# Split weight blocks at 17 start places, a backward and an alternating up projection in a two-layer encoder kernel

## The chip, the cores and the metric

The kernel runs on one core of a Trainium2 chip. Its time is the device time of one execution in microseconds, and lower is better. TensorE (PE) multiplies matrices, VectorE (DVE) and ScalarE (ACT) do elementwise work, GpSimd (POOL) a few memory sets, and SyncE (SP) issues the transfers.

## The reference

A trunk of two layers works on 512 tokens of width 1024, all in fp32. The first layer mixes tokens with differential attention, the second with chunked gated linear attention (GLA); beside it each layer attends to 256 memory tokens. Each layer ends with a gated MLP, which is where most of the change lies:

```python
def conv_ffn(h, w_up, conv_w, conv_b, w_down):
    u = h @ w_up                      # 1024 -> 2 * 2816
    c = depthwise causal convolution of width 3 over the tokens of u, + conv_b
    a, g = jnp.split(c, 2, axis=-1)
    return (jax.nn.silu(g) * a) @ w_down
...
for i in range(DEPTH):
    h = rms_norm(x, attn_norm[i])
    ...
    x = x + jnp.concatenate([mix, cross], axis=-1) @ w_out[i]
    h = rms_norm(x, ffn_norm[i])
    x = x + conv_ffn(h, w_up[i], conv_w[i], conv_b[i], w_down[i])
```

## The kernel before, in words

Everything is kept transposed: a tile has 128 features as partitions and the 512 tokens as columns, so an activation of width 1024 is eight tiles (k-tiles). Below, the first layer is `l = 0` in the code, the second `l = 1`.

**Split operands.** Each fp32 operand is written as a high part (rounded to the type float32r) and a low part (what is left), and a product is the sum of three matmuls: high by high, high by low, low by high. For weights, ACT casts the loaded block `raw` to `whi` (L253) and DVE subtracts to get `wlo` (L256); activations are split likewise into `xsh` and `xsl`.

**Weights as blocks.** All weights lie in DRAM as one row of blocks of 128 x 1024 or less, in the order of use. `_pieces` lists the pieces: four blocks for 512 columns of a projection, two for 256 columns of an up projection, three for 256 columns of a down projection over half of the hidden features. Three `raw` buffers are filled ahead by SP. The split parts have `WB` = 6 buffers each (L33, L286 and L474 for the first piece). `weights(key)` (L298) splits blocks so that the piece asked for and the one after it are there; in the projections `by_block` limits it to `WB` blocks, and `freed` (L307) splits one more when the last reader of a block has been issued.

**Two kinds of product.** In the projections of the token mixers (`gemm`, L330 to L332) the activation is the stationary operand and the weight block streams, 512 columns or 272. In the up, down and output projections (`product`, L351 to L353) 128 columns of the weight block are stationary and the 512 tokens of an activation stream into one PSUM bank: 8, 12 or 10 k-tiles of three matmuls each. PSUM has eight banks, two for each of the tags mm, sm, lg and tp.

**The MLP** (`ffn`, L1096). The 22 pairs of up tiles (a and g) are done in two halves of 6 and 5 weight pairs `q`, each with `n` = 0 and 1. For each `n`: the product a, the product g, then for both the convolution (`conv`, L1110: DVE L1111 empties the bank into `u`, ACT L1113, DVE L1114 and L1115), the silu (ACT L1146), the product of both (DVE L1147) and its split (ACT L1149, DVE L1150) into `midh` and `midl`. The tiles with n = 0 use the banks mm, those with n = 1 the banks sm. After the up tiles of a half come its eight down products over 12 or 10 mids, in their order, into banks lg and tp, each added to the residual (L1061).

**What sets the order.** TensorE keeps the order in which the code calls it; a hand-written script puts the units of the projections between the steps of attention. The order of ACT, DVE and SP is made by a scheduler at build time from dependencies and estimated costs and is then fixed: an instruction that waits holds all that stand behind it on its engine. A tile of a pool with all buffers in use waits until the readers of one of them are done.

Of the kernel before, what the change touches and what calls it, by code (L numbers as in the profile page):

```python
# [12 lines left out]
F32R = mybir.dt.float32r  # L13
# [16 lines left out]
WTILE = 1024  # L30
HALVES = (6, 5)
XS = 36
WB = 6  # L33

TOGETHER = (((0, 2), (0, 0)), ((0, 3),), ((0, 1), (1, 1)), ((1, 2), (1, 0)), ((1, 3),))
NT = 3 * len(TOGETHER)
# [143 lines left out]
def trunk(ctx, tc, head_d, x_t, mem_t, wpack, cols_a_d, cols_d, conv_d, gate_d, rel_bias, diff_lambda, consts, onehot, out):  # L180
# [86 lines left out]
    order = [(i, len(b[2]), b[4]) for i, piece in enumerate(blocks) for b in piece]  # L267
    first_of = [sum(len(q) for q in blocks[:i]) for i in range(len(blocks) + 1)]
    done, raw_q = [0], deque()

    def ahead():
        while len(raw_q) < 3 and done[0] + len(raw_q) < len(order):
# [3 lines left out]
    def make_block(raws=None):  # L276
        i, n, w = order[done[0]]
        if raws is None:
            ahead()
            raw = raw_q.popleft()  # L280
        else:
            raw = raws.pop(0)
        done[0] += 1
        while len(made) <= i:
            made.append([])
        hi, lo = (wp.tile([128, WTILE], F32R, name=t, tag=t, bufs=WB) for t in ("whi", "wlo"))  # L286
        split_weights(slice(0, n * w), raw, hi, lo, i == 2)
        made[i] += [(hi[:, blk(j, w)], lo[:, blk(j, w)]) for j in range(n)]
        if raws is None:
            ahead()  # L290
# [26 lines left out]
    def gemm(sh, sl, nb, key, w, evac, hook=None, late=False):  # L317
# [24 lines left out]
        for b, k in units:  # L342
            F.add(6 * w / 2370.0, lambda b=b, k=k: unit(b, k, k + 2))


    def product(p, parts, n, pairs, ids=None):
        ids = range(len(parts)) if ids is None else ids
        first, last = (ids[0], ids[-1]) if len(ids) == len(parts) else (0, len(parts) - 1)
        for i in ids:
            (hi, lo), (bh, bl) = parts[i], pairs[i]  # L350
            mm(p, hi[:, blk(n)], bh, start=i == first, stop=False)  # L351
            mm(p, hi[:, blk(n)], bl, start=False, stop=False)  # L352
            mm(p, lo[:, blk(n)], bh, start=False, stop=i == last)  # L353
# [83 lines left out]
    with tc.tile_pool(name="ini", bufs=1) as ip, tc.manual_schedule(engines={E.Activation, E.DVE, E.Pool, E.SP}):  # L437
        idle = ip.tile([128, 512], F32, name="idle")
        rb = ip.tile([32, 6], F32, name="rb")
        oh = ip.tile([32, 640], F32, name="oh")  # L440
        bs = xtile()[:6], xtile()[:6, :128]
        lv = xtile()[:, :256]
        G.memset(idle, 0.0)
        p = bank("tp")
        for n in (512, 320):
            mm(p[:, :n], idle[:, 0:128], idle[:, :n], start=True, stop=True)


        raws = [ip.tile([128, WTILE], F32, name=f"raw{i}") for i in range(4)]
        for t in (blk(0, S // 2), blk(1, S // 2)):  # L450
            A.dma_start(raws[0][:, t], wpack[0, :, t])
        head = ip.tile([128, 32 + S], F32, name="head")
        for c in (slice(0, 32 + S // 2), slice(32 + S // 2, 32 + S)):
            load(head[:, c], head_d[:, c])
        xT[0] = head[:, 32:]
        for k in range(1, KT):
            xT[k] = xtile()
            load(xT[k], x_t[k])
            load(raws[k // 2][:, blk(k % 2, S)], wpack[k // 2, :, blk(k % 2, S)])
        load(cols_a, cols_a_d)  # L460
        at[0] = 4
        load(C[:, 384:512], consts[:, 384:512])
        load(rb, rel_bias)
        load(oh, onehot)
        second = [load_raw(raw_tile(), WTILE) for _ in range(3)]
        load(cols, cols_d)
        load(lv, diff_lambda[0].rearrange("a b -> (a b)").partition_broadcast(128))
        parts, acc, split_w = [], [None], [None]
        made.append(parts)
        done[0] = 4  # L470

        def operands(k):
            if k % 2 == 0:
                split_w[0] = [wp.tile([128, WTILE], F32R, name=n, tag=n, bufs=WB) for n in ("whi", "wlo")]  # L474
            c = blk(k % 2, S)
            hi, lo = split_w[0]
            xh[k], xl[k] = split_tiles()
            if k == 0:
                for t in (blk(0, S // 2), blk(1, S // 2)):
                    V.tensor_copy(hi[:, t], raws[0][:, t])  # L480
                V.tensor_sub(lo[:, c], raws[0][:, c], hi[:, c].bitcast(F32))
                for t in (blk(0, S // 2), blk(1, S // 2)):
                    split(xh[0][:, t], xl[0][:, t], xT[0][:, t], col(0, head))
            else:
                split(xh[k], xl[k], xT[k], col(k, head))
                split_weights(c, raws[k // 2], hi, lo)
            parts.append((hi[:, c], lo[:, c]))
            squares(xT[k], acc)

        operands(0)  # L490
        for k in range(KT):
            if k + 1 < KT:
                operands(k + 1)
            if k == 0:
                second.append(load_raw(raws[0], WTILE))
            if k == 4:
                bias_rows(rb, oh, bs)
            if k == KT - 2:
                for j in range(4):
                    if j == 3:  # L500
                        token_rsqrt("lg", acc[0], NB, r_x[:, 0])
                    make_block(second)
                weights(("qk", 0), True)
                small_vectors()
                for c in range(2):
                    load(bias_d[:, 512 * c:min(512 * c + 512, 640)], bs[c])
            hi, lo = parts[k]
            terms = (xh[k], hi), (xh[k], lo), (xl[k], hi)
            full, left, right = slice(0, S), blk(0, S // 2), blk(1, S // 2)
            todo = [(b, i, full) for b in range(NB) for i in range(3)]  # L510
            if k == 0:
                todo = [(0, 0, left), (1, 0, left), (0, 0, right), (1, 0, right)] + sorted(
                    [u for u in todo if u[:2] not in ((0, 0), (1, 0))], key=lambda u: u[1])
            for b, i, t in todo:
                xp, w = terms[i]
                mm(first[b][:, t], xp[:, blk(b)], w[:, t], start=k == 0 and i == 0 and t is not right,
                   stop=k == KT - 1 and i == 2)
# [578 lines left out]
    def ffn(pool, l, acc):  # L1096
# [6 lines left out]
        def up(parts, n):  # L1103
            i = nu[0]
            nu[0] += 1
            p = bank("mm" if i % 4 < 2 else "sm")
            product(p, parts, n, list(zip(xh, xl)))
            return p, us[i % 4]

        def conv(p, u, j):  # L1110
            V.tensor_mul(u[:, 2:], p, rB)  # L1111
# [21 lines left out]
        for half, nq in enumerate(HALVES):  # L1133
            mids = []
            for q in range(base, base + nq):
                wa = weights(("ua", l, q))
                wg = None
                for n in range(2):
                    ua = up(wa, n)
                    wg = wg or weights(("ug", l, q))  # L1140
                    ug = up(wg, n)
                    if q == 0 and n == 0:
                        row_scales(acc[0])
                    ca = conv(*ua, 2 * q + n)
                    cg = conv(*ug, 22 + 2 * q + n)
                    A.activation(cg, cg, AF.Silu)  # L1146
                    V.tensor_mul(ca, ca, cg)  # L1147
                    mh, ml = split_tiles() if len(mids) < 5 else split_tiles(pool, "mid", 18)
                    A.copy(mh, ca)  # L1149
                    V.tensor_sub(ml, ca, mh.bitcast(F32))  # L1150
                    mids.append((mh, ml))
            last = half == 1
            if last and l == 0:
                tables("natural_log_exp_and_others")
            acc2 = [None]
            for c in range(4):
                pn = bank("lg"), bank("tp")
                parts = weights(("dn", l, base, c))
                for n in range(2):
                    product(pn[n], parts, n, mids)  # L1160
                for n in range(2):
                    if last and l == 1 and c == 3 and n == 1:
                        for t, queue in ((blk(0, S // 2), nc.sync), (blk(1, S // 2), nc.scalar)):
                            V.tensor_add(xT[7][:, t], xT[7][:, t], pn[n][:, t])
                            queue.dma_start(out[7, :, t], xT[7][:, t])
                        continue
                    update(2 * c + n, pn[n], (lambda k: c_attn(1, k)) if last and l == 0 else None, acc2)
                    if last and l == 0:
                        nc.sync.dma_start(xres[2 * c + n], xT[2 * c + n])
                    if last and l == 1:  # L1170
                        nc.sync.dma_start(out[2 * c + n], xT[2 * c + n])
            base += nq
# [88 lines left out]
```

## Time and profile before

| | |
|---|---|
| median of 2 runs | 1168.76 us (1168.76 to 1168.77) |
| profiled execution, first to last instruction | 1166.9 us |
| TensorE busy, matmuls | 1161.2 us, 5658 records |
| weight loads | 966.0 us |
| VectorE busy | 750.8 us |
| ScalarE busy | 545.6 us |
| bytes moved by the DMA queues | 117.68 MB, a mean of 101 GB/s |

The median lies 1.9 us above the span of the profiled execution, which counts from its first to its last instruction. Rows of a group read: line, engine, operation, output and inputs with their sizes, count, then busy time and mean duration of one in ns, then idle time before it. Rows of the timeline read: start, duration in us, engine, line, operation, tiles, count, and in brackets the idle time before it and what ended it. Rows of the windows read: stretch, its length, then busy time and count for PE, weight loads, DVE, ACT and POOL, the granted clock, the DMA share and GB/s. Plain fp32 matmuls have two records each.

### The profile page before, as it was taken

How to read it: one execution, taken by the hardware profiler on the slowest of the kernel's cores; microseconds unless marked ns; L12 is line 12 of the kernel's file. 1: busy time of each engine (PE TensorE's matmuls, PEld its weight loads, DVE VectorE, ACT ScalarE, POOL GpSimd, SP SyncE). 2: the span in 40 equal slices, each digit the busy share in tenths (PEclk: the TensorE clock that was granted, in tenths of full speed). 3: DMA queues.
4: the chain of work that ended last, by engine and by line, in shares of the span. 5: the costliest groups of instructions: out<-in, count | busy, mean ns of one | idle time of the engine just before them, and what ended most of it. 6: DMA issues, size and time to landing. Idle time of an engine off the chain costs nothing.

```text
span 1166.9 us, 14790 instructions
## 1 busy us (share of the span) xinstructions
PE 1161.2 (100%) x5658; PEld 966.0 (83%) x5658; DVE 750.8 (64%) x1256; ACT 545.6 (47%) x951; POOL 5.0 (0%) x27
## 2 busy tenths in 40 slices
PE   9999999999999999999999999999999999999998
PEld 7888888888888888888888888988888888888887
DVE  7576778688677326677447637777876743576741
ACT  6676787555344213344437634436643421343420
POOL 0000000000000000000000000000000000000000
PEclk9999999999999999999999999999999999999999
DMA  8522242234223223223341230333232333232231
GB/s 292 160 73 96 77 140 73 59 106 128 88 90 115 86 90 121 78 91 99 120 147 63 84 106 6 108 122 110 93 123 73 95 104 108 81 118 73 88 102 45
DMA packets 39556, 117.68 MB, mean 101 GB/s; under 512 B 4703, under 2 KB 7192, under 8 KB 39486
## 3 DMA queue, kind: packets, MB, share of 16 engines
q1 hardware_dynamic: 39054, 116.35, 30.9%
q8 instruction: 44, 0.72, 0.3%
q10 hardware_dynamic: 432, 0.39, 0.1%
q14 instruction: 26, 0.21, 0.1%
HBM read 112.52 MB, written 4.21 MB: 100 GB/s over the span
## 4 chain that ended last, share of the span: by engine, by line
PE 98%; ACT 1%; DVE 1%; issue 0%; POOL 0%; DVEq 0%; POOLq 0%
PE ps_mm L351 9%; PE ps_mm L352 9%; PE ps_mm L353 9%; PE ps_sm L352 8%; PE ps_sm L351 7%; PE ps_sm L353 7%; PE ps_mm L330 6%; PE ps_mm L332 6%; PE ps_mm L331 6%; PE ps_tp L351 3%; PE ps_lg L352 3%; PE ps_tp L352 3%; PE ps_lg L351 3%; PE ps_tp L353 3%; PE ps_lg L353 3%; PE ps_tp L220 3%
## 5 line engine op out<-in xcount | busy, mean ns | idle before, releaser
L253 ACT CAST whi<-raw 128x1024 fp32r<-128x1024 f32 (+4 forms) x212 | 207.7, 986 | 245.7 <-PE ps_tp L352 120.9
L256 DVE TENSOR_TENSOR wlo<-raw,whi 128x1024 fp32r<-128x1024 f32 (+4 forms) x212 | 240.3, 1139 | 117.6 <-ACT whi L253 116.7
L351 PE MATMUL ps_mm<-xsh,whi 128*128 128x512 f32 x438 | 171.6, 392 | 0.0
L353 PE MATMUL ps_mm<-xsh,wlo 128*128 128x512 f32 x438 | 170.5, 389 | 0.0
L352 PE MATMUL ps_mm<-xsl,whi 128*128 128x512 f32 x438 | 170.5, 389 | 0.0
L351 PE MATMUL ps_sm<-xsh,whi 128*128 128x512 f32 x378 | 147.0, 389 | 0.0
L352 PE MATMUL ps_sm<-xsl,whi 128*128 128x512 f32 x378 | 147.0, 389 | 0.0
L353 PE MATMUL ps_sm<-xsh,wlo 128*128 128x512 f32 x378 | 147.0, 389 | 0.0
L330 PE MATMUL ps_mm<-whi,xsh 128*128 128x512 f32 (+2 forms) x336 | 129.3, 385 | 0.0
L332 PE MATMUL ps_mm<-whi,xsl 128*128 128x512 f32 (+2 forms) x336 | 126.2, 375 | 0.0
L331 PE MATMUL ps_mm<-wlo,xsh 128*128 128x512 f32 (+2 forms) x336 | 125.8, 375 | 0.0
L1113 ACT ACTIVATE cvo<-u,cv 128x512 f32<-128x512 f32 x88 | 71.4, 815 | 112.1 <-DVE u L1111 112.1
L353 PEld LDWEIGHTS ps_mm<-xsh,wlo 128*128 128x128 f32 x438 | 82.2, 188 | 17.2
L351 PEld LDWEIGHTS ps_mm<-xsh,whi 128*128 128x128 f32 x438 | 82.2, 188 | 17.1 <-issue 0.3
L352 PEld LDWEIGHTS ps_mm<-xsl,whi 128*128 128x128 f32 x438 | 82.3, 188 | 17.0 <-DVE xsl L311 0.4
L1114 DVE SCALAR_TENSOR_TENSOR cvo<-u,cv,cvo 128x512 f32<-128x512 f32 x88 | 65.7, 748 | 36.2 <-ACT cvo L1113 36.0
L351 PEld LDWEIGHTS ps_sm<-xsh,whi 128*128 128x128 f32 x378 | 71.0, 188 | 14.8
L353 PEld LDWEIGHTS ps_sm<-xsh,wlo 128*128 128x128 f32 x378 | 71.0, 188 | 14.7
L352 PEld LDWEIGHTS ps_sm<-xsl,whi 128*128 128x128 f32 x378 | 71.0, 188 | 14.6
L332 PEld LDWEIGHTS ps_mm<-whi,xsl 128*128 128x128 f32 x336 | 63.2, 188 | 11.7
L330 PEld LDWEIGHTS ps_mm<-whi,xsh 128*128 128x128 f32 x336 | 63.2, 188 | 11.3 <-issue 0.3
L331 PEld LDWEIGHTS ps_mm<-wlo,xsh 128*128 128x128 f32 x336 | 63.3, 188 | 10.4
(295 smaller groups left out, 1760.8 us busy)
## 6 DMA issues: line engine op xcount, KB each, us to landing
raw<-in_wpack_dram SPq DMA_DIRECT2D x178, 512.0 KB, 3.5
xt<-in_x_t_dram SPq DMA_DIRECT2D x15, 256.0 KB, 5.4
raw<-in_wpack_dram SPq DMA_DIRECT2D x15, 256.0 KB, 3.1
raw<-in_wpack_dram SPq DMA_DIRECT2D x8, 384.0 KB, 3.1
xres<-xt SPq DMA_DIRECT2D x8, 256.0 KB, 2.7
xt<-xres SPq DMA_DIRECT2D x8, 256.0 KB, 6.2
out_dram<-xt SPq DMA_DIRECT2D x7, 256.0 KB, 2.0
bt<-bias_d SPq DMA_DIRECT2D x6, 256.0 KB, 4.4
```

Source lines behind the costliest of these rows:

```text
L220: nc.tensor.transpose(dst, src, ident[:n, :n])
L253: ins = A.copy(hi[:, c], raw[:, c])
L256: V.tensor_sub(lo[:, c], raw[:, c], hi[:, c].bitcast(F32))
L330: mm(p, sh[k][:, blk(b)], hi, start=k == 0, stop=False)
L331: mm(p, sh[k][:, blk(b)], lo, start=False, stop=False)
L332: mm(p, sl[k][:, blk(b)], hi, start=False, stop=k == KT - 1)
L351: mm(p, hi[:, blk(n)], bh, start=i == first, stop=False)
L352: mm(p, hi[:, blk(n)], bl, start=False, stop=False)
L353: mm(p, lo[:, blk(n)], bh, start=False, stop=i == last)
L1113: A.activation(c, u[:, 2:], AF.Identity, scale=cv[l][:, 2, j:j + 1], bias=cv[l][:, 3, j:j + 1])
L1114: V.scalar_tensor_tensor(c, u[:, 1:S + 1], cv[l][:, 1, j:j + 1], c, op0=ALU.mult, op1=ALU.add)
```

## The change

It does four things. The split parts of each weight block lie in a tile of 1024 + 64 columns and begin at one of 17 columns in turn (0, 4, ... 64, that is 16 bytes apart), the same place for `whi` and `wlo`. `WB` falls from 6 to 5. In the second layer the up tiles with n = 1 (a and g) read each streamed operand from its last token to its first and write the bank in the same reversed order, so that each result lands where it did. In the first layer the a and g products with n = 1 are issued together: for each k-tile and each of the three terms the matmul of a, then that of g, into the two banks sm in turn.

```diff
-WB = 6
+WB = 5
+PLACES = tuple(4 * i for i in range(17))
...
+    places = cycle(PLACES)
+
+    def weight_tiles():
+        c = next(places)
+        return [wp.tile([128, WTILE + max(PLACES)], F32R, name=n, tag=n, bufs=WB)[:, c:c + WTILE] for n in ("whi", "wlo")]
...
-        hi, lo = (wp.tile([128, WTILE], F32R, name=t, tag=t, bufs=WB) for t in ("whi", "wlo"))
+        hi, lo = weight_tiles()
...
+    def back(t):
+        return t[:, ::-1]
+
+    def product_back(p, parts, n, pairs):
+        for i in range(len(parts)):
+            (hi, lo), (bh, bl) = parts[i], pairs[i]
+            mm(back(p), hi[:, blk(n)], back(bh), start=i == 0, stop=False)
+            mm(back(p), hi[:, blk(n)], back(bl), start=False, stop=False)
+            mm(back(p), lo[:, blk(n)], back(bh), start=False, stop=i == len(parts) - 1)
+
+    def products(p2, parts2, n, pairs):
+        for i in range(len(pairs)):
+            bh, bl = pairs[i]
+            for t, x in ((0, bh), (0, bl), (1, bh)):
+                for p, parts in zip(p2, parts2):
+                    mm(p, parts[i][t][:, blk(n)], x, start=i == 0 and t == 0 and x is bh,
+                       stop=i == len(pairs) - 1 and t == 1)
...
-            product(p, parts, n, list(zip(xh, xl)))
+            if l == 1 and n == 1:
+                product_back(p, parts, n, list(zip(xh, xl)))
+            else:
+                product(p, parts, n, list(zip(xh, xl)))
             return p, us[i % 4]
+
+        def up2(parts, n):
+            i = nu[0]
+            nu[0] += 2
+            p = [bank("mm" if i % 4 < 2 else "sm") for _ in range(2)]
+            products(p, parts, n, list(zip(xh, xl)))
+            return [(p[0], us[i % 4]), (p[1], us[i % 4 + 1])]
...
-                    ua = up(wa, n)
-                    wg = wg or weights(("ug", l, q))
-                    ug = up(wg, n)
+                    if l == 0 and n == 1:
+                        ua, ug = up2((wa, wg), n)
+                    else:
+                        ua = up(wa, n)
+                        wg = wg or weights(("ug", l, q))
+                        ug = up(wg, n)
```

The first piece's tiles (L474) come from `weight_tiles` as well.

More of the change, by code (lines that the diff above doesn't have):

```diff
@@ L473, in operands @@
             if k % 2 == 0:
-                split_w[0] = [wp.tile([128, WTILE], F32R, name=n, tag=n, bufs=WB) for n in ("whi", "wlo")]
+                split_w[0] = weight_tiles()
             c = blk(k % 2, S)
```

## The prediction

> **What bounds the kernel now.** I read the page first (busy time, clock, the chain that ended last), then the groups, then the timeline of TensorE and of the engines that feed it.
>
> ```profile
> span 1166.9 us, 14790 instructions
> ...
> PE 1161.2 (100%) x5658; PEld 966.0 (83%) x5658; DVE 750.8 (64%) x1256; ACT 545.6 (47%) x951; POOL 5.0 (0%) x27
> ...
> PEclk9999999999999999999999999999999999999999
> ...
> PE 98%; ACT 1%; DVE 1%; issue 0%; POOL 0%; DVEq 0%; POOLq 0%
> ...
> L351 PE MATMUL ps_mm<-xsh,whi 128*128 128x512 f32 x438 | 171.6, 392 | 0.0
> ...
> L353 PEld LDWEIGHTS ps_mm<-xsh,wlo 128*128 128x128 f32 x438 | 82.2, 188 | 17.2
> ```
>
> TensorE is busy for the whole span, the chain lies on it for 98%, and it is granted its full clock throughout. So the time is the number of matmuls times the step from one start to the next, plus the few places where TensorE waits. The duration of 392 ns is not that step, because matmuls overlap; the step comes from starts in the timeline. The weight load of 188 ns lies beside the matmul before it.
>
> ```profile
> 299.62 0.39 PE L352 MATMUL ps_sm<-xsl,whi 128*128 128x512 f32 x1
> ...
> 305.97 0.39 PE L353 MATMUL ps_sm<-xsh,wlo 128*128 128x512 f32 x1
> ...
> 374.65 0.39 PE L353 MATMUL ps_sm<-xsh,wlo 128*128 128x512 f32 x1
> 374.88 0.39 PE L351 MATMUL ps_lg<-xsh,whi 128*128 128x512 f32 x1
> ...
> 613.30 0.29 PE L330 MATMUL ps_lg<-whi,xsh 128*128 128x272 f32 x1
> ...
> 616.20 0.29 PE L332 MATMUL ps_lg<-whi,xsl 128*128 128x272 f32 x1
> 616.32 0.46 PE L330 MATMUL ps_mm<-whi,xsh 128*128 128x512 f32 x1
> ...
> 728.01 0.82 PE L1015 MATMUL ps_sm<-gv,xt 128*128 128x192 f32 x4
> 728.66 0.49 PE L1017 MATMUL ps_sm<-st,qx 96*128 96x192 f32 x2
> ...
> 803.00:1109.00 306.00, 306.00 (x1352) 253.38 (x1351) 197.87 (x247) 125.10 (x153) 0.00 (x0) 1.00 0.30 95
> ```
>
> From 299.62 to 305.97 stand 29 matmuls of 512 columns, 28 steps: 6.35/28 = 0.227 us each. The last row is the second layer's MLP up to its last up tile: 306/1352 = 0.226 us, so nothing but that step is in it. The 24 matmuls of 272 columns from 613.30 to 616.32 give 0.126 us. Two widths give a line: (227 - 126)/240 = 0.42 ns a column, and 227 - 512 x 0.42 = 12 ns that do not depend on the width. Four plain fp32 matmuls of 192 columns take 0.65 us from 728.01 to 728.66, 0.163 us each, 0.85 ns a column: the slowest streaming rate that this trace shows, twice the split operands' 0.42.
>
> **The change, part by part.** The count of matmuls, weight loads, casts, subtractions and transfers is unchanged; starts, directions and order move.
>
> *Seventeen start places.* Every split block starts 0 to 256 bytes into a tile 256 bytes longer. I take nothing for it. For whi as streamed operand the 272-wide blocks already start at 0, 272 and 544 columns, odd multiples of 64 bytes, and keep the one step of 0.126 us. For whi as stationary operand no row shows an odd start; the load's 188 ns may grow by 39 ns before it fills the step of 227. Below nothing lie at most the 12 ns of every product matmul; above, a load of double length, 376 - 227 = 149 ns on each of 3552, 529 us, to which I give no chance, because the same columns of the same partitions are read. Nearest is the 272-wide row: no change. Casts and subtractions write to shifted starts on engines that are 47% and 64% busy.
>
> *Backwards in the second layer.* The second 128 columns of each up tile, 11 pairs x 2 products x 8 k-tiles x 3 terms = 528 matmuls, read the moving operand and write the bank from the last column to the first. No matmul before does so. Below nothing: 528 x 12 ns = 6 us of gain. Above: the rate of the 192-wide row, 0.42 ns more for each of 512 columns, 215 ns, x 528 = 114 us. I take nothing: neighbours in the bank and in SBUF still follow each other, only in the other order, and the nearest row is the forward matmul of the same shape. Both ends go into the range or the rivals.
>
> The Trainium skill ("PSUM — Partial Sum Buffer", Specifications) states that any non-contiguous access pattern slows matmuls significantly, because PSUM's lines are 8 bytes. Whether a step of minus one counts as that, it does not say; if it does, the sum is the upper end above, and no run yet shows it.
>
> *Alternating in the first layer.* In the 11 up tiles with n = 1, the a and g products become one run of 48 matmuls that change bank at every step. At 374.65 to 374.88 the bank changes, and the step is 0.23 us as ever: alternation itself costs and brings nothing. What it moves is the end of the a product: it ends with g's, 5.4 us (24 x 0.227) later. Both banks of tag sm ended their last tiles two products, 10.9 us, before, so the start is not held. In the middle of an MLP half nothing waits for the tile; at the end of a half the down projection needs it 33 matmuls later (12 mids, the last one third to wait) and in the second half 27 later.
>
> ```profile
> 374.89 1.05 ACT L253 CAST whi<-raw 128x1024 fp32r<-128x1024 f32 x1 [1.71 <-PE ps_sm L352]
> 375.87 0.82 ACT L1113 ACTIVATE cvo<-u,cv 128x512 f32<-128x512 f32 x1
> ...
> 375.08 0.69 DVE L1111 TENSOR_TENSOR u<-ps_sm,rB 128x512 f32<-128x512 f32 x1 [0.17 <-PE ps_sm L353]
> 375.98 1.23 DVE L256 TENSOR_TENSOR wlo<-raw,whi 128x1024 fp32r<-128x1024 f32 x1 [0.21 <-ACT whi L253]
> 377.12 0.75 DVE L1114 SCALAR_TENSOR_TENSOR cvo<-u,cv,cvo 128x512 f32<-128x512 f32 x1
> 377.91 0.75 DVE L1115 SCALAR_TENSOR_TENSOR cvo<-u,cv,cvo 128x512 f32<-128x512 f32 x1
> 379.36 0.69 DVE L1147 TENSOR_TENSOR cvo<-cvo 128x512 f32<-128x512 f32 x1 [0.70 <-ACT cvo L1146]
> ...
> 380.08 0.62 ACT L1149 CAST midh<-cvo 128x512 fp32r<-128x512 f32 x1 [0.76 <-DVE cvo L1147]
> ...
> 380.73 0.69 DVE L1150 TENSOR_TENSOR midl<-cvo,midh 128x512 fp32r<-128x512 f32 x1 [0.69 <-ACT midh L1149]
> ...
> 382.36 0.39 PE L351 MATMUL ps_lg<-midh,whi 128*128 128x512 f32 x1
> 382.58 0.39 PE L352 MATMUL ps_lg<-midl,whi 128*128 128x512 f32 x1
> ...
> 548.98 0.62 ACT L253 CAST whi<-raw 128x512 fp32r<-128x512 f32 x1 [1.71 <-PE ps_sm L352]
> 549.95 0.82 ACT L1113 ACTIVATE cvo<-u,cv 128x512 f32<-128x512 f32 x1 [0.35 <-DVE u L1111]
> ...
> 550.80 0.75 DVE L1114 SCALAR_TENSOR_TENSOR cvo<-u,cv,cvo 128x512 f32<-128x512 f32 x1 [0.35 <-ACT cvo L1113]
> ...
> 553.76 0.62 ACT L1149 CAST midh<-cvo 128x512 fp32r<-128x512 f32 x1 [0.76 <-DVE cvo L1147]
> ...
> 554.41 0.69 DVE L1150 TENSOR_TENSOR midl<-cvo,midh 128x512 fp32r<-128x512 f32 x1 [0.69 <-ACT midh L1149]
> ...
> 555.08 0.39 PE L351 MATMUL ps_lg<-midh,whi 128*128 128x512 f32 x1
> 555.30 0.40 PE L352 MATMUL ps_lg<-midl,whi 128*128 128x512 f32 x1
> ```
>
> Today a's convolution is done while g streams, and only g's is left: midl is ready at 381.42, needed at 382.58, a margin of 1.2 us; in the second half ready at 555.10, needed at 555.30, 0.2 us. After the change both stand behind the last up matmul. In the built program's order ACT then runs two weight casts (their buffers come free at that moment) ahead of the first convolution, and DVE runs two L1111, a subtraction, four convolution steps, a subtraction, L1147 and L1150.
>
> First half: the casts issue every 0.98 us (374.89 to 375.87), so the first convolution starts at 376.85 and ends at 377.67; L1114 starts 0.6 us later than at 377.12. Two more convolution steps add 2 x 0.77 = 1.5. Ahead of L1147 the second subtraction (about 1.15) takes the place of the 0.70 wait for the silu: 0.45. Together 2.6: midh ready at 383.3 for 382.36, a stall of 0.9; then midl at 384.0, when TensorE wants it at 383.5: 0.5 more. 1.4 us. Second half: two casts of 1024 columns from 548.98 put the convolution at 550.94, 1.0 us after 549.95; again 1.5 and 0.45, together 3.0: midh ready at 557.4 for 555.08, a stall of 2.3, and 0.5 for midl. 2.8 us. The second layer's MLP keeps its order there and its zero stall. Sum: 4.2 us; 0 to 7 if those offsets were all hidden or the subtractions fell worse.
>
> *Five buffers for six.* A block's cast waits for a release that is one block later; behind a waiting cast stand ACT's softmax exponentials, evacuations and convolutions, and behind those the tiles that TensorE needs. By the built order the shortest way from a release to the first use of the block that now takes the buffer is 25 matmuls. Its tightest place is in the second layer's projections:
>
> ```profile
> 641.82 0.39 PE L332 MATMUL ps_mm<-whi,xsl 128*128 128x512 f32 x1
> ...
> 645.26 2.03 ACT L253 CAST whi<-raw 128x1024 fp32r<-128x1024 f32 x2
> ...
> 646.40 2.35 DVE L256 TENSOR_TENSOR wlo<-raw,whi 128x1024 fp32r<-128x1024 f32 x2
> ...
> 647.73 0.39 PE L331 MATMUL ps_mm<-wlo,xsh 128*128 128x512 f32 x1
> ```
>
> The release is at 641.82, ACT gets to the cast at 645.26 behind the softmax, half of the pair of subtractions ends at 647.6, and the low part is wanted at 647.73. It just holds: I take nothing, with up to 3 us if such places miss by some tenths. In the MLP the shortest way is 40 matmuls, 9 us, against some 3 for cast and subtraction.
>
> Sum: 1166.9 + 4.2 = 1171.1 for the span. The median of the runs, 1168.76, lies 1.9 above that span; 1171.1 + 1.9 = 1173.0.
>
> **The rivals.**
> - *Backwards streaming runs at the slower rate.* Place: 528 matmuls of the second layer's MLP; price 215 ns each. It decides against my forecast from 36 ns a matmul on (19 us beside the 4.2, the 2% mark). 1173 + 114 = 1287. For it: no row shows a reversed pattern. Against: same neighbours, same line. A part of it (50 ns) gives 1199.
> - *Weights starve.* At the 641.82 place the margin is 0.1 us; the two layers have some twenty piece boundaries in their projections, and 1 us each gives 1193. Against: all other leads exceed 25 matmuls.
> - *It is faster.* The 12 ns that do not depend on width belong to where stationary blocks start. All 3552 product matmuls (2112 up, 1056 down, 384 output) lose them: 43 us, 1173 - 43 = 1130, and from 8 ns on it is past 2%. For it: 12 ns stand in every step. Against: the 272-wide rows carry the same 12 ns at other starts. The Trainium skill ("TensorE: Matmul & The Clock Gate", Wait — 56ns, not 53.3ns?) gives about 216 ns for 512 columns where this trace has 227; by it, 11 x 3552 = 39 us would be to be had.
> - *Nothing happens*: the stalls are hidden, 1169.
>
> **How the numbers follow.** Forecast 0.71; nothing 0.03; starving 0.03; backwards at the slow rate 0.15; a part of it 0.05; faster 0.03. The range 1164 to 1225 takes in forecast, nothing, starving and the part, 0.82; the forecast alone is 1169 to 1178. A difference under 2%, 1145.4 to 1192.1, is about what a measurement of this kernel can tell from no change. Faster 0.02 (of the 0.03, the cases above 8 ns); slower 0.22 (slow rate, part, most of starving); same 0.76.
>
> **What would show it.** Right: steps of 227 ns on the backward, alternating and shifted matmuls alike; TensorE gaps of 1 to 3 us, ended by midh and midl, in the first down product of each half of the first layer's MLP, none in the second's. Wrong: a longer step on the backward tiles alone, a longer or shorter step that goes with the block's start, or waits on wlo in the projections.

## The result and the profile after

The changed kernel takes 1195.18 us (median of 2 runs, 1194.26 and 1196.11) against 1168.76: ratio 1.0222, 95% interval 1.0206 to 1.0239. That is 26.4 us slower, and 22 above the forecast of 1173.0, though inside the range. The profiled execution took 1194.26 us; its span grew from 1166.9 to 1192.5, by 25.6.

The page of the changed kernel, the rows that answer to those shown of before (the last two are groups: instructions, then busy time and mean ns of one):

```profile
PE 1183.9 (99%) x5658; PEld 966.6 (81%) x5658; DVE 747.5 (63%) x1256; ACT 542.8 (46%) x951; POOL 5.0 (0%) x27
...
PEclk9999999999999999999999999999999999999999
...
L375 PE MATMUL ps_mm<-xsh,whi 128*128 128x512 f32 x438 | 173.7, 397 | 0.0
...
L377 PEld LDWEIGHTS ps_mm<-xsh,wlo 128*128 128x128 f32 x438 | 82.3, 188 | 19.3
```

The same 5658 matmuls keep TensorE busy for 1183.9 us instead of 1161.2, at full clock. Nothing else got longer: VectorE and ScalarE work no more than before. A weight load takes 188 ns as ever. The matmul of L375 reads 397 ns where L351 read 392.

Where does TensorE wait?

```profile
PE ps_tp L221 <- DVE o L803: 1.3, 1, 1.3
...
PE ps_lg L375 <- ACT midh L1186: 1.1, 1, 1.1
PE ps_lg L376 <- DVE midl L1187: 0.4, 2, 0.2
```

These are the three largest waits that before did not have (total us, times, longest). Together they make 2.8 us, a ninth of the loss. So the rest is in the step. Two windows of the MLPs, 400 to 540 us in the first layer and 900 to 1100 in the second, show it; the columns are the window, its length, TensorE's busy time and in brackets the matmuls in it. Before:

```profile
400.00:540.00 140.00, 140.00 (x619) 1.00 0.30 92
...
900.00:1100.00 200.00, 200.00 (x884) 1.00 0.29 94
```

After:

```profile
400.00:540.00 140.00, 140.00 (x607) 1.00 0.28 94
...
900.00:1100.00 200.00, 200.00 (x863) 1.00 0.28 95
```

140/619 = 0.226 us a matmul has become 140/607 = 0.231, and 200/884 = 0.226 has become 200/863 = 0.232. The second window holds backward tiles, the first holds alternating ones, but neither is needed for a longer step. Here are two up products of the changed kernel with 24 forward matmuls each, in the old order (the first and the last row of each):

```profile
298.74 0.39 PE L375 MATMUL ps_mm<-xsh,whi 128*128 128x512 f32 x1
...
303.95 0.40 PE L377 MATMUL ps_mm<-xsh,wlo 128*128 128x512 f32 x1
...
343.04 0.39 PE L375 MATMUL ps_mm<-xsh,whi 128*128 128x512 f32 x1
...
348.40 0.39 PE L377 MATMUL ps_mm<-xsh,wlo 128*128 128x512 f32 x1
```

The first product has its two weight blocks at 0 and at 256 bytes: 23 steps in 5.21 us, 0.2265 each. The second has them at 112 and 128 bytes: 5.36/23 = 0.2330.

In the built programs every activation tile, and before the change every weight tile, begins 160 bytes above a multiple of 256. So before, the stationary and the moving operand of a matmul begin at the same place within 256 bytes, and now they do at 2 of the 17 places only. I call the difference of the two starts, counted within 256 bytes, their distance. Mean steps from start to start of matmuls of 512 columns, gaps above 0.3 us left out, before and after:

| matmuls | before | after | lost |
| --- | --- | --- | --- |
| projections (803) | 227.8 ns | 232.1 ns | 3.5 us |
| products, forwards (2467) | 226.8 ns | 231.1 ns | 10.7 us |
| products, alternating (528) | 226.8 ns | 232.2 ns | 2.9 us |
| products, backwards (528) | 226.8 ns | 234.2 ns | 3.9 us |

That is 21.0 us. The gaps above 0.3 us grew by 2.0, the first piece lost 0.3, and 2.3 of the 25.6 lie at narrower matmuls and transposes, where the wait of 1.3 for `o` stands. Among the forward products the step is 227.0 ns at distance 0, 227.2 at 16, 229.9 at 176 and 192, 228.5 at 240, and 231.5 to 234.2 at the others.

My theory from here on (the start theory): a step of 227 ns needs the two operands to begin at the same place within 256 bytes; elsewhere it is some 233. Rivals: the backward and alternating tiles slow TensorE beyond themselves; the wider tiles or the missing buffer do; the start of the weights alone counts; changing the start from block to block counts.

### The profile page after: what moved, and what is told of

Its sections match the earlier page's. It is cut to its first block, busy times and chain, and to the rows that moved or that the text cites. A ratio compares the mean times of both kernels' runs of the same rounds, so it can differ in the third digit from the quotient of the medians.

```text
span 1192.5 us, 14724 instructions
## 1 busy us (share of the span) xinstructions
PE 1183.9 (99%) x5658; PEld 966.6 (81%) x5658; DVE 747.5 (63%) x1256; ACT 542.8 (46%) x951; POOL 5.0 (0%) x27
## 4 chain that ended last, share of the span: by engine, by line
PE 96%; DVE 3%; ACT 1%; issue 0%; DMA 0%; DVEq 0%
PE ps_sm L367 10%; PE ps_mm L375 9%; PE ps_mm L377 9%; PE ps_mm L376 9%; PE ps_mm L336 6%; PE ps_mm L337 6%; PE ps_mm L338 6%; PE ps_sm L360 3%; PE ps_sm L359 3%; PE ps_sm L358 3%; PE ps_tp L377 3%; PE ps_tp L375 3%; PE ps_tp L376 3%; PE ps_lg L376 3%; PE ps_lg L377 3%; PE ps_lg L375 3%
## 5 line engine op out<-in xcount | busy, mean ns | idle before, releaser
L254 ACT CAST whi<-raw 128x1024 fp32r<-128x1024 f32 (+4 forms) x212 | 205.0, 982 | 259.4 <-PE ps_tp L376 131.4
L375 PE MATMUL ps_mm<-xsh,whi 128*128 128x512 f32 x438 | 173.7, 397 | 0.0
L375 PEld LDWEIGHTS ps_mm<-xsh,whi 128*128 128x128 f32 x438 | 82.3, 188 | 18.9 <-issue 0.3
L1148 DVE SCALAR_TENSOR_TENSOR cvo<-u,cv,cvo 128x512 f32<-128x512 f32 x88 | 64.9, 749 | 29.8 <-ACT cvo L1147 29.5
L360 PE MATMUL ps_sm<-xsh,wlo 128*128 128x512 f32 x176 | 70.0, 398 | 0.0
L359 PE MATMUL ps_sm<-xsl,whi 128*128 128x512 f32 x176 | 69.9, 397 | 0.0
L358 PE MATMUL ps_sm<-xsh,whi 128*128 128x512 f32 x176 | 69.9, 397 | 0.0
L1149 DVE SCALAR_TENSOR_TENSOR cvo<-u,cv,cvo 128x512 f32<-128x512 f32 x88 | 65.0, 750 | 2.1
L1183 ACT ACTIVATE cvo<-cvo 128x512 f32<-128x512 f32 x44 | 27.8, 631 | 62.1 <-DVE cvo L1149 62.1
L367 PE MATMUL ps_sm<-xsh,whi 128*128 128x512 f32 x176 | 55.2, 395 | 0.0
```

The costliest lines, as they stand in the source:

```text
L254: ins = A.copy(hi[:, c], raw[:, c])
L358: mm(back(p), hi[:, blk(n)], back(bh), start=i == 0, stop=False)
L359: mm(back(p), hi[:, blk(n)], back(bl), start=False, stop=False)
L360: mm(back(p), lo[:, blk(n)], back(bh), start=False, stop=i == len(parts) - 1)
L367: mm(p, parts[i][t][:, blk(n)], x, start=i == 0 and t == 0 and x is bh, stop=i == len(pairs) - 1 and t == 1)
```

## The experiments

Before ran beside them at 1169.04, 1168.88 and 1168.75 us (medians on the chips of the three sets).

**Only the places.** All tiles forwards, one product after the other, five buffers:

```diff
-            if l == 1 and n == 1:
+            if False:
...
-                    if l == 0 and n == 1:
+                    if False:
```

> Only the seventeen places and the five buffers are kept; all up tiles stream forwards, one product after the other. The start theory (the step from one matmul to the next is 227 ns where the stationary and the moving operand begin at the same place within 256 bytes, and some 233 ns where they don't) expects nearly the whole loss: the forward products of the changed kernel stepped by 231.1 ns for 226.8, 3523 x 4.4 = 15.4 us, and its projections lost 3.5 us, so 1168.8 + 19 = 1188, with steps of 227 ns at the first place and at the one 256 bytes on. The rival that the backward and the alternating tiles slow TensorE expects 1169. The forecast on record (places cost nothing) expects 1169 too.

1190.81 us, ratio 1.0185 [1.0170, 1.0201]. The windows:

```profile
400.00:540.00 140.00, 140.00 (x607) 1.00 0.28 95
...
900.00:1100.00 200.00, 200.00 (x866) 1.00 0.27 95
```

The step is 0.231 us in both layers without a backward or an alternating matmul. 21.8 of the 26.4 us are here (2.9 of them are the missing buffer's, see below), and the first rival falls as the main cause. By distance the forward products again step by 227.1 ns at 0, by 227.5 at 16, by 231 to 234 from 32 to 160.

**Only backwards.** From here on the changed lines of the last diff stay as they are there unless named.

```diff
-WB = 5
-PLACES = tuple(4 * i for i in range(17))
+WB = 6
+PLACES = (0,)
...
             if l == 1 and n == 1:
```

> Only the backward streaming in the second layer is kept, with six buffers and every block at the start of its tile. The start theory has the moving operand begin at its last column, 4 bytes short of the same place, and expects 528 longer steps, of about 233 ns: 528 x 6.5 = 3.4 us, 1172. The rival that backward streaming is the main cause expects 1185 or more, with long steps on other matmuls too. The forecast on record (backwards costs nothing) expects 1169.

1172.99 us, ratio 1.0038 [1.0024, 1.0053]. A forward product and the backward one behind it:

```profile
809.89 0.39 PE L375 MATMUL ps_mm<-xsh,whi 128*128 128x512 f32 x1
...
815.10 0.39 PE L377 MATMUL ps_mm<-xsh,wlo 128*128 128x512 f32 x1
...
815.78 0.40 PE L358 MATMUL ps_sm<-xsh,whi 128*128 128x512 f32 x1
...
821.15 0.40 PE L360 MATMUL ps_sm<-xsh,wlo 128*128 128x512 f32 x1
```

Forwards 5.21/23 = 0.2265 us, backwards 5.37/23 = 0.2335. Over all 528 the mean is 233.4 ns, 6.6 more than forwards: 3.5 us, and the other matmuls keep their step.

**Only alternating.**

```diff
-WB = 5
-PLACES = tuple(4 * i for i in range(17))
+WB = 6
+PLACES = (0,)
...
                     if l == 0 and n == 1:
```

> Only the alternation between two banks in the first layer is kept. The forecast on record expects two waits of TensorE at the ends of that layer's MLP halves, 1.4 and 2.8 us, 1173. The start theory expects steps of 227 ns throughout, so that the waits are as long as the forecast had them, for the longer steps of the changed kernel no longer hide them: 1171 to 1173. The rival that changing the bank at every matmul slows it (232 ns for 227 on 528 matmuls) expects 2.8 us beside the waits, 1176.

1171.62 us, ratio 1.0022 [1.0012, 1.0031]. The 528 alternating matmuls step by 226.7 ns, so a change of bank at every matmul costs nothing. The ends of the two halves:

```profile
382.47 0.49 PE L375 MATMUL ps_lg<-midh,whi 128*128 128x512 f32 x1
383.19 0.50 PE L376 MATMUL ps_lg<-midl,whi 128*128 128x512 f32 x1 [0.23 <-DVE midl L1187]
383.53 0.40 PE L377 MATMUL ps_lg<-midh,wlo 128*128 128x512 f32 x1
...
555.59 0.39 PE L377 MATMUL ps_lg<-midh,wlo 128*128 128x512 f32 x1
556.84 0.49 PE L375 MATMUL ps_lg<-midh,whi 128*128 128x512 f32 x1 [0.86 <-ACT midh L1186]
557.57 0.50 PE L376 MATMUL ps_lg<-midl,whi 128*128 128x512 f32 x1 [0.23 <-DVE midl L1187]
557.91 0.40 PE L377 MATMUL ps_lg<-midh,wlo 128*128 128x512 f32 x1
```

What a start lies later than one step of 0.227 is the stall: 0.49 + 0.11 = 0.6 us in the first half, 1.02 + 0.50 + 0.11 = 1.6 in the second. 2.2 us together, at the places that the prediction named and for midh and midl as it said, but not the 4.2.

**Five buffers of the wider tile, one place.**

```diff
-PLACES = tuple(4 * i for i in range(17))
+PLACES = (0,)
...
-        return [wp.tile([128, WTILE + max(PLACES)], F32R, name=n, tag=n, bufs=WB)[:, c:c + WTILE] for n in ("whi", "wlo")]
+        return [wp.tile([128, WTILE + 64], F32R, name=n, tag=n, bufs=WB)[:, c:c + WTILE] for n in ("whi", "wlo")]
```

> Five buffers of the wider tile (4352 bytes), every block at the first place, nothing backwards, nothing alternating. The start theory expects the time of before, 1169, with a step of 227 ns. The rival that the wider tiles or the missing buffer slow TensorE expects about 1188, and steps of 231 ns.

1171.97 us, ratio 1.0022 [1.0012, 1.0033]; the product step is 226.8 ns. So the wide tile does not lengthen the step, but 2.9 us are lost, which I had expected to be nothing. They are the missing buffer's and not the wider tile's: the kernel with both operands moved, below, has five buffers of the narrow tile, takes 2.7 us more than before and shows the same wait of 1.3 us. One place of the loss can be seen. This kernel:

```profile
214.48 1.06 ACT L254 CAST whi<-raw 128x1024 fp32r<-128x1024 f32 x1
...
215.57 1.23 DVE L257 TENSOR_TENSOR wlo<-raw,whi 128x1024 fp32r<-128x1024 f32 x1 [0.77 <-ACT whi L254]
...
218.03 0.69 DVE L803 TENSOR_TENSOR o<-ps_sm,rs 128x512 f32<-128x512 f32 x1
...
218.86 0.63 PE L221 MATMUL ps_tp<-C,o 128*128 128x128 f32 x4 [1.33 <-DVE o L803]
```

Before, at the same place:

```profile
213.83 0.42 ACT L253 CAST whi<-raw 128x256 fp32r<-128x256 f32 x1
...
214.28 0.43 DVE L256 TENSOR_TENSOR wlo<-raw,whi 128x256 fp32r<-128x256 f32 x1
...
215.41 0.69 DVE L779 TENSOR_TENSOR o<-ps_sm,rs 128x512 f32<-128x512 f32 x1
```

With a buffer fewer each block is cast later, so another block's cast falls into the norm between the attention and its output: 1024 columns instead of 256 (1.06 for 0.42 us, its subtraction 1.23 for 0.43). From the cast's start to the scaling of `o` it is 3.55 us instead of 1.58, and TensorE waits 1.3. The same wait stands in the changed kernel's list. The rest of the 2.9 us I can't assign to a place: no other new wait in the list is above 0.3.

**The weights moved by 128 bytes, no places.** One place, and a pad between the two pools:

```diff
-PLACES = tuple(4 * i for i in range(17))
+PLACES = (0,)
...
     xs = ctx.enter_context(tc.tile_pool(name="xs", bufs=1))
+    pad_w = ctx.enter_context(tc.tile_pool(name="pad_w", bufs=1)).tile([128, 32], F32, name="pad_w")
     wp = ctx.enter_context(tc.tile_pool(name="wp", bufs=2))
```

> No places, five buffers, nothing backwards or alternating; a pad of 128 bytes a partition ahead of the weight pool (and of all pools behind it) moves every split weight block by 128 bytes, and leaves the activations ahead of it where they were. So 3888 matmuls of 512 columns take stationary and moving operand from starts 128 bytes apart, and 624, whose activations lie behind the weights and move along, don't. The start theory expects steps of 233 ns on the 3888 and of 227 ns on the 624: 2930 x 6.7 + 958 x 5.5 = 25 us beside the time of the five buffers alone, 1172 + 25 = 1197. The rival that it is the seventeen different starts, one after the other, that cost, and not the start itself, expects 1172.

1193.67 us, ratio 1.0211 [1.0196, 1.0226].

```profile
400.00:540.00 140.00, 140.00 (x605) 1.00 0.29 95
```

One place for all blocks, and the step is 0.231 us again: it isn't the change of place from block to block. The 624 product matmuls whose activations moved along step by 228.2 ns, the other forward ones by 232.8. The 228.2 is a mean over two parts: the first five steps behind matmuls at 128 bytes are 229 to 235 ns on average, the ones behind them 226.8.

**Both moved by 128 bytes.**

```diff
+    pad_x = ctx.enter_context(tc.tile_pool(name="pad_x", bufs=1)).tile([128, 32], F32, name="pad_x")
     xs = ctx.enter_context(tc.tile_pool(name="xs", bufs=1))
     wp = ctx.enter_context(tc.tile_pool(name="wp", bufs=2))
```

> The pad of 128 bytes lies ahead of the activation pool, so that activations and weights both move by 128 bytes and begin at the same place within 256 bytes again, though at another than before. The start theory (only the distance of the two starts counts) expects 227 ns and 1172, the time of five buffers alone. The rival that each block's own start within 256 bytes counts expects 233 ns and 1197.

1171.61 us, ratio 1.0030 [1.0020, 1.0040].

```profile
400.00:540.00 140.00, 140.00 (x619) 1.00 0.29 92
```

**The activations moved by 128 bytes, the weights by 256.**

```diff
+    pad_x = ctx.enter_context(tc.tile_pool(name="pad_x", bufs=1)).tile([128, 32], F32, name="pad_x")
     xs = ctx.enter_context(tc.tile_pool(name="xs", bufs=1))
+    pad_w = ctx.enter_context(tc.tile_pool(name="pad_w", bufs=1)).tile([128, 32], F32, name="pad_w")
     wp = ctx.enter_context(tc.tile_pool(name="wp", bufs=2))
```

> A pad of 128 bytes ahead of the activations and another ahead of the weights: the activations move by 128 bytes, the weights by 256, which is the same place within 256 bytes as before. The start theory expects the same 25 us as from the moved weights, 1197, with 233 ns on 3888 matmuls and 227 ns on 624. The rival that the start of the weight blocks alone counts expects 1172.

1194.02 us, ratio 1.0213 [1.0198, 1.0228].

```profile
400.00:540.00 140.00, 140.00 (x605) 1.00 0.30 95
```

605, 619, 605: weights alone, both, activations alone. It isn't either operand's own start that costs, but their distance.

**A map of 64 places.**

```diff
-PLACES = tuple(4 * i for i in range(17))
+PLACES = tuple(range(64))
```

> 64 places, 4 bytes apart, in turn; five buffers, nothing backwards or alternating. A map of the step against the distance of the two starts. The start theory expects 227 ns at 0 and 16 bytes and between them, some 230 ns about 176 to 192, 233 ns elsewhere, and about 1191. Two readings of the backward tiles are told apart by the distance of 4 bytes on either side of 0: if backward streaming is slow because its first column lies 4 bytes short of the same place, forward matmuls with that distance (252 or 4 bytes) step by 233 ns; if it is slow because the columns come in falling order, they step by 227 to 229 ns.

1194.44 us, ratio 1.0217 [1.0197, 1.0237]. Most distances give 230 to 236 ns, as expected. But the map isn't the one I had in mind: 16 bytes, 227.2 ns in the changed kernel, gives 233.4 here; 100, 120, 156 and 252 bytes give 226.6 to 227.5; and 0 itself gives 228.6, with single steps up to 236. The last has the reason seen with the 624 matmuls: blocks at distance 0 come behind others, and the first steps are still long. At 382.47 such a stretch begins; to 383.40 four steps take 0.93 us, from there to 384.99 seven take 1.59, which is 0.227 each. At 4 bytes the step is 232.4, at 252 226.6, so the question about the backward tiles was left to the next two kernels.

**Backwards, all blocks at 252 bytes.**

```diff
-PLACES = tuple(4 * i for i in range(17))
+PLACES = (63,)
...
             if l == 1 and n == 1:
```

> The backward up tiles of the second layer are kept; every split weight block begins 252 bytes into its tile, five buffers. A backward stream begins 4 bytes below its neighbour's start, so with 252 bytes (4 short of 256) its stationary operand begins at the same place within 256 bytes as its first column. Forward matmuls at a distance of 252 bytes stepped by 226.6 ns in the map of places, so they stay as they were. If the backward tiles step by 233 ns because of where they begin, they step by 227 ns here: 1172, the time of five buffers alone. If they do because their columns come in falling order, they keep 233 ns: 528 x 6.6 = 3.5 us more, 1175 to 1176.

1185.44 us, ratio 1.0141 [1.0125, 1.0158]: neither. The backward tiles keep 233.3 ns at this start too, so the longer step goes with the falling order. But the forward matmuls, which the map had at 226.6, now step by 226.7 in the MLP of one layer and by 233.3 in that of the other (the second window holds backward ones too):

```profile
400.00:540.00 140.00, 140.00 (x620) 1.00 0.29 93
...
900.00:1100.00 200.00, 200.00 (x859) 1.00 0.29 94
```

140/620 = 0.226, 200/859 = 0.233, at one distance. The moment of a switch can be seen:

```profile
253.07 0.40 PE L375 MATMUL ps_mm<-xsh,whi 128*128 128x512 f32 x1
...
258.44 0.40 PE L377 MATMUL ps_mm<-xsh,wlo 128*128 128x512 f32 x1
258.67 0.39 PE L1158 MATMUL ps_tp<-xsh 128*128 128x512 f32 x1
258.90 0.39 PE L1159 MATMUL ps_tp<-xsl,xsh 128*128 128x512 f32 x1
259.13 0.39 PE L375 MATMUL ps_sm<-xsh,whi 128*128 128x512 f32 x1
...
264.34 0.39 PE L377 MATMUL ps_sm<-xsh,wlo 128*128 128x512 f32 x1
```

24 matmuls in 5.37 us, 0.2335 a step; then two matmuls whose stationary operand is an activation tile, at distance 0; then 24 in 5.21 us, 0.2265 a step, on the same activations as the 24 ahead of the switch, and on the two weight blocks that had stepped by 0.2333 from 247.47 to 252.84. From there on the short step holds for 300 us, up to the first down product of the second half, where TensorE waits for `midl`: 0.48 us from 559.01 to 559.49, in place of 0.227. Behind this wait the step is the long one again:

```profile
559.01 0.39 PE L375 MATMUL ps_lg<-midh,whi 128*128 128x512 f32 x1
559.49 0.50 PE L376 MATMUL ps_lg<-midl,whi 128*128 128x512 f32 x1
...
560.06 0.40 PE L375 MATMUL ps_tp<-xsh,whi 128*128 128x512 f32 x1
...
564.96 0.40 PE L375 MATMUL ps_tp<-midh,whi 128*128 128x512 f32 x1
```

21 steps in 4.90 us, 0.2333 each, and so it stays to the end of that MLP. The kernel of five buffers at distance 0 has the same wait at the same place:

```profile
557.13 0.39 PE L375 MATMUL ps_lg<-midh,whi 128*128 128x512 f32 x1
557.61 0.50 PE L376 MATMUL ps_lg<-midl,whi 128*128 128x512 f32 x1
...
559.10 0.39 PE L376 MATMUL ps_tp<-xsl,whi 128*128 128x512 f32 x1
...
563.63 0.39 PE L375 MATMUL ps_tp<-midh,whi 128*128 128x512 f32 x1
```

There the steps behind the wait are 229 to 235 ns up to 558.87, and from 559.10 on 20 steps take 4.53 us, 0.2265 each. So at distance 0 the short step comes back by itself after a few matmuls. At 252 bytes there are two steps, 226.7 and 233.3 ns, both lasting, and which one holds depends on what went before.

**Reading backwards alone.** As in the kernel that was only backwards, with six buffers and one place, but:

```diff
-            mm(back(p), hi[:, blk(n)], back(bh), start=i == 0, stop=False)
-            mm(back(p), hi[:, blk(n)], back(bl), start=False, stop=False)
-            mm(back(p), lo[:, blk(n)], back(bh), start=False, stop=i == len(parts) - 1)
+            mm(p, hi[:, blk(n)], back(bh), start=i == 0, stop=False)
+            mm(p, hi[:, blk(n)], back(bl), start=False, stop=False)
+            mm(p, lo[:, blk(n)], back(bh), start=False, stop=i == len(parts) - 1)
```

> Only the reading of the backward tiles is backwards; the bank is written forwards, so those tiles come out with their columns in reverse order. Six buffers, one place. If the longer step of the backward tiles comes from reading the activations while a weight block is loaded, it stays: 233 ns on 528 matmuls, 1172 to 1173. If it comes from writing the bank backwards, it goes: 227 ns and 1169.

1172.61 us, ratio 1.0031 [1.0018, 1.0044].

```profile
815.41 0.40 PE L358 MATMUL ps_sm<-xsh,whi 128*128 128x512 f32 x1
...
820.78 0.40 PE L360 MATMUL ps_sm<-xsh,wlo 128*128 128x512 f32 x1
```

5.37/23 = 0.2335 us, exactly the step of the whole backward tile. All of it comes from the reading, none from the bank.

**All blocks at 16 bytes.**

```diff
-PLACES = tuple(4 * i for i in range(17))
+PLACES = (4,)
...
-        return [wp.tile([128, WTILE + max(PLACES)], F32R, name=n, tag=n, bufs=WB)[:, c:c + WTILE] for n in ("whi", "wlo")]
+        return [wp.tile([128, WTILE + 64], F32R, name=n, tag=n, bufs=WB)[:, c:c + WTILE] for n in ("whi", "wlo")]
```

> All split weight blocks begin 16 bytes into their tile; five buffers, nothing backwards or alternating. At this distance the kernel of seventeen places stepped by 227.5 ns and the map of 64 places by 233.4 ns. If the distance alone sets the step, as the first of these has it: 227 ns and 1172. If 16 bytes are a distance like any other and something else made the step short there (the place that came before it was 0, a good one): 233 ns on 3552 product matmuls and some 231 ns on the projections, 1172 + 23 = 1195.

1187.60 us, ratio 1.0160 [1.0145, 1.0176]: again between the two.

```profile
400.00:540.00 140.00, 140.00 (x602) 1.00 0.29 94
...
900.00:1100.00 200.00, 200.00 (x884) 1.00 0.30 95
```

The reverse of 252 bytes: 0.233 in the first layer's MLP, 0.226 in the second's. So 16 bytes allow both steps too. And here as well the short one ends at a wait for `midl` (0.48 us, 1132.20 to 1132.68), behind which it is 233.3.

**The whole change, two places 256 bytes apart.**

```diff
-PLACES = tuple(4 * i for i in range(17))
+PLACES = (0, 64)
```

Backward and alternating tiles and the five buffers stay as in the changed kernel.

> The whole change, but with two places 256 bytes apart for the seventeen 16 bytes apart. The start theory expects the loss to fall to what the parts beside the places cost: 1169.0 + 2.9 (five buffers) + 3.9 (backwards) + 2.6 (alternating) = 1178, with steps of 227 ns on forward and alternating matmuls and 233 ns on the backward ones. The rival that moving starts from block to block cost by themselves expects 1190 or more.

1177.33 us, ratio 1.0073 [1.0058, 1.0088], for 1178 expected.

```profile
400.00:540.00 140.00, 140.00 (x620) 1.00 0.28 92
...
900.00:1100.00 200.00, 200.00 (x875) 1.00 0.31 96
```

0.226 us in the first layer; in the second 0.229, a mixture of 226.9 forwards and 233.4 backwards. So the 17 places 16 bytes apart cost 1195.2 - 1177.3 = 17.9 us beside the other three parts, which cost 8.6. Without the backward and alternating tiles it is 1190.8 - 1172.0 = 18.8. No variant came below the time before.

## Why the prediction was wrong, step by step

The range, 1164 to 1225, holds the measured 1195; the forecast of 1173 and its main step do not hold.

- **What bounds the kernel** was right: TensorE's step, at full clock. The whole loss is read in the terms it gave, the step and a few waits. One row was misread: the four rows of 192 columns are two plain fp32 matmuls of two records each, so 0.85 ns a column is the rate of a record, not of a matmul. It was used for the price of the backward rival alone.
- **The step that failed: "Seventeen start places ... I take nothing for it."** It measured 17.9 us. The bounds held the price (about 4.4 ns a product matmul, between -12 and +149), but I put no chance on it, and no rival has it. Two arguments misled. First, I looked for the price in the weight load and its 39 ns of room; the load still takes 188 ns in the changed kernel, and the step grew all the same, so the room was beside the point. Second, I took the 272-wide row as the nearest. Its blocks lie at 0, 64 and 128 bytes within 256 (not all at odd multiples of 64), and their one step was read rightly, but it does not carry over to 512 columns: in all fourteen kernels the 272-wide matmuls keep a median step of 124 to 127 ns, whatever their distance. The effect that cost 17.9 us does not show at that width. "The same columns of the same partitions are read" was the wrong exclusion: at 512 columns it counts where they lie against the other operand.
- **Backwards, "I take nothing"**: 6.6 ns a matmul, 3.5 to 4 us of time. The rivals at 215 and 50 ns a matmul did not occur. The Trainium skill's rule on non-contiguous patterns ("PSUM — Partial Sum Buffer", Specifications) does not show for a bank written with a step of minus one: with the bank written forwards the step is the same 0.2335 us.
- **Alternating, "costs and brings nothing"** was right, 226.7 ns.
- **The ends of the halves**: right place, right tiles, size off: 0.6 + 1.6 = 2.2 us alone for 1.4 + 2.8. In the alternating kernel's timeline the first convolution of the first half starts at 376.39, not 376.85; in the second half one of the two casts is of 512 columns, not 1024 (the pair takes 1.57 us from 549.22); and in the first half the four convolution steps take 2.75 us (377.28 to 380.03), where I had before's two with 1.54 and twice 0.77 more.
- **Five buffers, nothing, "up to 3"**: 2.9 us by the medians. The place I watched, the second layer's projections, was not the place; the visible wait is behind the first layer's attention, where not a late weight but a longer cast in the norm's chain does it.
- **The rival "faster"**: no distance stepped below 226.6 ns on average in any kernel, so none of the starts tried brings any of the 12 ns beside the width.
- **The chances**: 0.76 lay on no difference, and it is 2.2% slower. That the range held the time is luck: it was stretched for backward streaming at a part of the slow rate, which is not what happened. The sign I had listed, "a longer or shorter step that goes with the block's start", is what the trace shows.

What stays open: what the two operands collide on. It is not a longer load: the load begins some 3 ns behind a matmul's start and takes 188 ns with either step (192 for a third of them in the first layer at 16 bytes). The longer step appears with the distance of two starts, and it appears when the activations are read in falling order, not when a bank is written so. That fits two reads of SBUF by TensorE, stream and next weight block, which meet at the same place in turn; it is argued, not shown. The Trainium skill ("TensorE: Matmul & The Clock Gate", Step-by-step: what each phase is for) gives TensorE two independent read ports, one for each operand; the padded kernels do not fit full independence, as their steps of 227 and 233 ns differ by the distance of the two operands alone. Also open is what switches the step at a distance other than 0. A wait of TensorE ended the short one both times that it was lost in an MLP; the long one gave way at 252 bytes to a pair of matmuls at distance 0 (258.67) and at 16 bytes to a row of transposes (from 795.62 on); but the same pair left the kernel with 16 bytes at the long step. And why 272 columns show nothing of it, no run tells.

## What to carry to other kernels

Where a kernel runs at TensorE's step, let the stationary and the moving operand of a matmul begin at the same place within 256 bytes: a pad or a slice of 64 fp32 columns was free here at 512 streamed columns, others could cost 6 to 7 ns of 227 a matmul. Look at the step between starts by window, and not at one short stretch or at another width, before calling a layout free: where the starts differ, one wait was enough here to turn the short step into the long one for the rest of a stage. A buffer taken away can cost at a place where no weight is late, when a longer cast lands in a short chain of another stage.

## What the runs showed of the hardware that I had not expected

- Two steps for the same matmul of 512 columns, 226.7 and 233.3 ns. The 6.7 ns between them are the time of 16 columns at the 0.42 ns a column worked out in the prediction. With all starts alike the short one held: in the first layer's window 619 or 620 matmuls in 140 us in all seven kernels with distance 0 there, the one before among them, and 602 to 607 in those at 16 bytes, at 128 bytes, with 17 and with 64 places. The 233.3 is a mean: at 128 bytes single steps of 229 and 238 ns take turns.
- At a distance other than 0 either step lasts: at 252 bytes it stayed at 226.7 ns from 260 to 559 us and at 233.3 from 800 us to the end. At distance 0 the step is back at 227 ns some five matmuls after a wait or after matmuls at another distance.
- Reading the moving operand from the last column to the first: 233.4 ns, with the weight blocks at 0 and at 252 bytes alike.
